# One encoder layer on one core: the mixer's output projection as seven half-size products in place of eight

## The chip, the cores and the metric

The kernel runs on one core of one Trainium2 chip. The metric is the device time of one execution in microseconds, given as the median of several runs. The profile is one more execution, recorded instruction by instruction. TensorE (PE) multiplies matrices, VectorE (DVE) and ScalarE (ACT) work element by element, GpSimd (POOL) does so as well and issues the DMAs that add one block in SBUF to another, and SyncE (SP) issues nearly all other DMAs.

## The reference

One layer over 512 rows of width 1024, in float32:

```python
u = rms_norm(h, g_mix[i])
z = u @ w_in[i]
...
gates = jax.nn.sigmoid(gate_logits).reshape(B, S, N_BRANCH, D_MODEL)
mixed = gates[:, :, 0] * y_a + gates[:, :, 1] * y_b
h = h + mixed @ w_mix_out[i]
u = rms_norm(h, g_mlp[i])
h = h + jnp.square(jax.nn.relu(u @ w_ff1[i])) @ w_ff2[i]
ple_gate = jax.nn.sigmoid(rms_norm(h, g_ple[i]) @ w_ple_gate[i])
h = h + ple_gate * (p[i] @ w_ple_proj[i])
```

`y_a` and `y_b` are two attention branches, each 512x512, projected to 1024 columns. The line that changes is `mixed @ w_mix_out[i]`, a product of 512x1024 with 1024x1024. A last RMS norm ends the layer.

## The kernel before

Every matrix product is done in three matmuls: each operand is split into a high part, rounded by ACT to TensorE's fast float32 format, and a low part, which DVE finds by subtracting (`hi_lo`, L68). `mm3` (L73) multiplies high by high, high by low and low by high. Weights are split in the same way, one "unit" of 128x1024 at a time (`emit_split`, L301). A list `order` holds all units in the order in which TensorE uses them; `advance` (L328) splits units up to a number, and `look["n"]` is the next one. Each unit's weights come from a "raw" block that SP loads into one of a few places. A planner (L189 to L226) gives each raw block the place that comes free first, and `emit_dma` (L246) issues a load only when the split of the last unit that used the place before has been issued. PE and POOL run in the order in which the program is written; ACT and DVE do so only inside `manual_schedule` blocks, and elsewhere the tile framework orders them.

Two parts of the layer already use Strassen's scheme in Winograd's form: the right half of each of the two gates and the MLP. There a product of 2x2 blocks takes seven block products in place of eight, numbered 1, 2, 5, 6, 7, 3 and 4. Their operands are sums of blocks. The sums of weights are made in place by `sum_source` (L276): POOL issues a DMA that adds one raw block to another (L298), or DVE adds them (L296). Product 5's weights are block 00 plus block 01; product 6's are those plus block 11; 7's are block 01 plus block 11, in place of block 01; 4's are those of 6 plus block 10. So each sum waits until the split of the unit before it has read the block. The results are gathered in three PSUM banks x, y and z: 6, 7 and 4 are added into the bank of 1, and 3 into that of 5, so the outputs are taken from the banks as they stand at that moment.

The stages around the change, in TensorE's order, are:

- branches 0 to 3 (`branches`, L1003): 24 matmuls for each block of 128 columns; DVE multiplies the PSUM results by the gates (L1016), adds the two (L1017) and splits the sum into an operand of the output projection (`mix_t`, L895);
- 14 gate products (`win_mm`, L906), then branches 4 to 7;
- the output projection, 8 output tiles of 128x512. For each, `row_group` (L1059) runs over 8 row blocks of `w_mix_out`, 3 matmuls each. `h2` (L1190) adds the tile to h (`h_add`, L1070) and lets ACT square it (`part_ssq`, L1081). When both halves of a 128-row block are done, `scale2` (L1194) finds 1/rms on POOL and scales the block on DVE, `t2_pe` (L1133) transposes it on PE, and `t2_top` (L1158, blocks 0 and 1) or `t2_sums` and its successors (L1166 to L1188, blocks 2 and 3) make the MLP's operands out of it;
- `pp_half` (L1210): the PLE projection `p @ w_ple_proj`, 8 tiles of 6 matmuls. It lies between the last tile of the output projection and the MLP, with the transposes of blocks 2 and 3 among it;
- the MLP: `steps` (L112) is a list of products in the order of `STEPS` (L46), where a and b are the first and second of a pair of 512 hidden columns in the first matrix (24 matmuls of 128x256 a product), A and B the same in the second (12 of 128x512).

The raw blocks of the output projection were 4 of 1 MB. The first MLP block had a place of its own ("t2"), free from the start of the projection.

Of the kernel before, what the change touches and what calls it, by code (L numbers as in the profile page):

```python
# [45 lines left out]
STEPS = "a1 b1 a2 a5 b5 b2 a6 b6 a7 a3 b7 b3 A1 a4 b4 B1 A2 A5 B5 B2 A6 B6 A3 A7 B7 B3 A4 B4"  # L46
ET = mybir.EngineType
# [3 lines left out]
def layer_kernel(ctx: ExitStack, tc: tile.TileContext, x, p, g_mix, w_in, b_forget, swa_sinks,  # L51
# [52 lines left out]
    def block(w, r0, c0, nk, nc_, name):  # L104
# [8 lines left out]
             for fq in range(4) for c, pn in STEPS.split()]  # L113
# [44 lines left out]
    for half in range(2):  # L158
        for r4 in range(2):
            for j, u in enumerate(rows(w_mix_out, r4 * 512, half * 512, f"wmix{half}{r4}")):  # L160
                add(("mix", half, 2 * r4 + j), u)
    for half in range(2):
        add(("pp", half), rows(w_ple_proj, 0, half * 512, f"wpp{half}", 2)[0])
    first_ff = len(raws)
    ff_blocks = {}
    for g in range(8):
        ff_blocks["f1", g] = block(w_ff1, 0, g * 512, 4, 256, f"wf1_{g}")
        ff_blocks["s2", g] = block(w_ff2, g * 512, 0, 2, 512, f"wf2_{g}")
# [61 lines left out]
    def ff_place(pl, shape):  # L230

        key = pl[:2] if isinstance(pl, tuple) else pl
        if key not in ff_tiles:
            if isinstance(pl, tuple):

                for z in range(2):
                    ff_tiles[pl[0], z] = (look["wp2"] if pl[0] else wp).tile(
                        [P, 2, 1024], F32, tag="w2_raw" if pl[0] else "w_raw", bufs=2,
                        name=f"wq{z}")
# [6 lines left out]
    def emit_dma(i):  # L246

        upto = max(first_raw[r] for r in raws_of(i))
        while look["d"] <= upto:
# [4 lines left out]
            if first_ff <= r_ < last_ff:  # L254
                if "place" not in look:
                    return
# [19 lines left out]
    def sum_source(i):  # L276
# [22 lines left out]
        sources[i] = q if key[0] == "s2" else q.rearrange("q k (j c) -> q k j c", c=P)  # L299

    def emit_split(i):  # L301
# [19 lines left out]
        for a in range(np_):  # L321
# [3 lines left out]
            nc.vector.tensor_tensor(lo[:, z], src[:, z], hi[:, z].bitcast(F32), ALU.subtract)  # L325
# [567 lines left out]
    mix = [None] * 8  # L893

    def mix_t(m):  # L895

        for i in (m // 2, 4 + m // 2):
            if mix[i] is None:
                mix[i] = at2.tile([P, 2, S], F32R, tag=f"d{i}", name=f"mix_{i}")
        return mix[m // 2][:, m % 2], mix[4 + m // 2][:, m % 2]  # L900

# [101 lines left out]
    def branches(m):  # L1003
# [8 lines left out]
        for i in range(2):  # L1012
            ps = mm_tile(f"psy{i}_{m}")
# [3 lines left out]
        nc.vector.tensor_tensor(sig[0], sig[0], sig[1], ALU.add)  # L1017
        hi_lo(*mix_t(m), sig[0])
# [3 lines left out]
    for t in P2_STEPS:  # L1022
# [12 lines left out]
        for n in range(look["n"], i + 9):  # L1035
            sum_source(n)
# [481 lines left out]
```

## Time and profile before

| | |
|---|---|
| median of 3 runs | 716.11 us (715.39 to 716.51) |
| span of the profiled execution | 715.3 us, granted clock 0.997 |
| PE busy | 704.4 us, 98% |
| DVE, ACT, POOL busy | 532.7, 450.2 and 84.8 us |
| DMA | 115.67 MB, 162 GB/s in the mean |

The profiled execution has no time of its own beside its span. The span runs from the first to the last instruction; the runs' median lies 0.8 us above it. Rows of the trace give the start, the duration, the engine, the line in the kernel and the operation as output<-inputs; `[... <-X]` is how long the engine stood idle before it and what ended that. A matmul's recorded duration overlaps the next one's, so its cost is the distance between starts. Weight units are named by number: u43 to u50 are those of the output projection before, with h for the high and l for the low part.

### The profile page before, as it was taken

The page shows a single profiled execution, that of the slowest core. Times are in us where ns is not written, and L with a number is a line of the kernel's source. Part 1 is how long each engine was busy: PE and PEld are TensorE (multiplying, and loading weights), DVE is VectorE, ACT ScalarE, POOL GpSimd, SP SyncE. Part 2 cuts the span into 40 slices and gives each one's busy share as a digit, 9 for nine tenths or more (in the row PEclk, how much of TensorE's full clock was granted, in tenths as well). Part 3 has the DMA queues.
Part 4 walks back from the last instruction along what each step waited for, and adds up shares of the span by engine and source line. Part 5 has one row for each costly group of instructions (what it writes and reads, how often), then busy time and mean ns, then how long its engine had stood idle before and what let it go on. Part 6 is the DMA issues. An engine that isn't in the chain of part 4 may idle for free.

```text
span 715.3 us, 11466 instructions
## 1 busy us (share of the span) xinstructions
PE 704.4 (98%) x4229; PEld 626.4 (88%) x4229; DVE 532.7 (74%) x908; ACT 450.2 (63%) x839; POOL 84.8 (12%) x124
## 2 busy tenths in 40 slices
PE   8999999999999999999999999999999999999995
PEld 7988888888888998888899889988999789988885
DVE  6557888877696556545789985899579966997565
ACT  6547888779863554344788736874477546875452
POOL 1011211100001200001510102010300021010101
PEclk9999999999999999999999999999999999999998
DMA  9256456670364795450885598739894699079002
GB/s 288 70 164 159 115 125 158 151 196 1 119 206 118 147 320 181 152 172 31 238 188 193 111 288 160 239 86 256 185 253 119 152 243 233 34 148 351 3 22 96
DMA packets 74055, 115.67 MB, mean 162 GB/s; under 512 B 6664, under 2 KB 44560, under 8 KB 74000
## 3 DMA queue, kind: packets, MB, share of 16 engines
q1 hardware_dynamic: 65936, 86.24, 38.0%
q0 software_dynamic: 7776, 28.32, 21.5%
q8 instruction: 33, 0.54, 0.3%
q10 hardware_dynamic: 288, 0.39, 0.2%
q14 instruction: 22, 0.18, 0.1%
HBM read 72.93 MB, written 4.19 MB: 108 GB/s over the span
## 4 chain that ended last, share of the span: by engine, by line
PE 86%; DVE 6%; DMA 4%; issue 2%; ACT 1%; POOL 0%; SPq 0%; POOLq 0%; DVEq 0%; ACTq 0%
PE pf L74 5%; PE pf L76 5%; PE pf L75 5%; PE s_6x L1331 3%; PE s_0x L1331 3%; PE h_sc L760 3%; PE s_2x L1331 2%; PE h_pv L830 2%; PE h_tr L818 2%; PE psm L76 2%; PE psm L74 2%; PE psy L74 2%; PE psy L75 2%; PE psm L75 2%; PE psy L76 2%
## 5 line engine op out<-in xcount | busy, mean ns | idle before, releaser
L298 POOL DMA_DIRECT2D wq<-wq x24 | 21.8, 936 | 166.8 <-DVE u70l L325 25.9
L778 ACT ACTIVATE s<-s,h_nm 128x128 f32<-128x128 f32 (+1 forms) x64 | 32.6, 512 | 5.9 <-DVE h_nm L771 5.1
L71 DVE TENSOR_TENSOR h_ptl<-h_tr,h_pth 128x512 fp32r<-128x512 f32 (+2 forms) x40 | 22.9, 604 | 4.0 <-ACT h_pth L70 3.6
L359 POOL TENSOR_SCALAR n_ms<-acc 128x1 f32<-128x1 f32 x15 | 5.6, 373 | 163.8 <-ACT junk L1083 105.4
L70 ACT CAST h_pth<-h_tr 128x512 fp32r<-128x512 f32 (+2 forms) x40 | 19.4, 523 | 1.8 <-PE h_tr L818 1.4
L70 ACT CAST u<-n_tr 128x512 fp32r<-128x512 f32 (+2 forms) x26 | 12.6, 519 | 11.8 <-PE n_tr L1139 5.6
L474 PE MATMUL va<-wv_h,u 128*128 128x320 f32 x64 | 20.0, 317 | 0.0
L818 PE MATMUL h_tr<-ident,s 128*128 128x128 f32 x136 | 19.6, 277 | 0.2
L474 PE MATMUL vb<-wv_h,u 128*128 128x328 f32 x64 | 19.6, 313 | 0.0
L71 DVE TENSOR_TENSOR u<-n_tr,u 128x512 fp32r<-128x512 f32 (+2 forms) x26 | 15.0, 603 | 5.8 <-ACT u L70 5.7
L298 POOL DMA_DIRECT2D wgw<-wgw x8 | 7.1, 971 | 102.3 <-DVE u25l L325 77.7
L1083 ACT ACTIVATE junk<-h_sb 128x512 f32<-128x512 f32 x16 | 10.1, 630 | 12.6 <-DVE h_sb L1073 10.1
L830 PE MATMUL h_pv<-h_pth,v 128*128 128x256 f32 (+1 forms) x64 | 17.3, 291 | 0.0
L830 PE MATMUL h_pv<-h_ptl,v 128*128 128x256 f32 (+1 forms) x64 | 16.9, 305 | 0.3 <-DVE h_ptl L71 0.3
L818 PEld LDWEIGHTS h_tr<-ident,s 128*128 128x128 f32 x136 | 15.1, 141 | 2.0 <-ACT s L798 0.5
L1420 DVE TENSOR_TENSOR sgp<-sgp,pp 128x512 f32<-128x512 f32 (+1 forms) x9 | 5.7, 632 | 14.2 <-ACT sgp L1419 14.2
L1073 DVE TENSOR_TENSOR h_sb<-psm,h_sb 128x512 f32<-128x512 f32 x8 | 5.5, 689 | 13.8 <-PE psm L76 13.8
L798 ACT ACTIVATE s<-s,h_rec 128x128 f32<-128x128 f32 (+2 forms) x32 | 14.2, 483 | 2.4 <-DVE h_rec L792 2.4
L840 DVE TENSOR_TENSOR h_ao<-h_pv,h_ao 64x512 f32<-64x512 f32 x16 | 10.9, 681 | 6.0 <-ACT h_ao L839 5.8
L766 DVE CUSTOM_DVE_ANT_0 s<-h_sc,causal 128x128 f32<-128x128 f32 (+3 forms) x32 | 13.8, 483 | 0.3 <-PE h_sc L760 0.3
L792 DVE RECIPROCAL h_rec<-h_den 128x4 f32<-128x4 f32 x16 | 3.0, 185 | 14.5 <-ACT s L778 14.3
L830 PEld LDWEIGHTS h_pv<-h_ptl,v 128*128 128x128 f32 x64 | 12.1, 188 | 1.7 <-DVE h_ptl L71 0.8
(1609 smaller groups left out, 2774.9 us busy)
## 6 DMA issues: line engine op xcount, KB each, us to landing
wq<-in_w_ff_dram SPq DMA_DIRECT2D x45, 512.0 KB, 5.9
wq<-wq POOLq DMA_DIRECT2D x24, 512.0 KB, 5.9
wq_c<-in_w_ff_dram SPq DMA_DIRECT2D x9, 512.0 KB, 6.7
wg<-in_w_in_dram SPq DMA_DIRECT2D x4, 1024.0 KB, 5.3
wgw<-in_w_in_dram SPq DMA_DIRECT2D x8, 512.0 KB, 4.7
wgw<-wgw POOLq DMA_DIRECT2D x8, 512.0 KB, 5.8
wmix<-in_w_mix_out_dram SPq DMA_DIRECT2D x4, 1024.0 KB, 5.1
wpg<-in_w_ple_gate_dram SPq DMA_DIRECT2D x4, 1024.0 KB, 8.6
```

Source lines behind the costliest of these rows:

```text
L70: nc.scalar.copy(hi, src)
L71: nc.vector.tensor_tensor(lo, src, hi.bitcast(F32), ALU.subtract)
L74: nc.tensor.matmul(ps, lh, rh, start=start, stop=False)
L75: nc.tensor.matmul(ps, lh, rl, start=False, stop=False)
L76: nc.tensor.matmul(ps, ll, rh, start=False, stop=stop)
L298: nc.gpsimd.dma_start(q, other, accum_op=ALU.add)
L474: nc.tensor.matmul(ps, u[:, kk_, ts_], w[:, kk_, c0:c1], start=kk_ == 0 and n == 0, stop=kk_ == KT - 1 and n == 2)
L760: nc.tensor.matmul(ps[:, off:off + n], qs[i][z][:, qb * P:(qb + 1) * P], kk[i][z][:, k0:k0 + n], start=z == 0, stop=z == 1)
L778: nc.scalar.activation(sl, sl, AF.Exp, bias=nm[:, qb:qb + 1], accum_out=den[:, qb:qb + 1])
L818: nc.tensor.transpose(tr[:, n, :], c["s"][:, o, :], ident)
L830: nc.tensor.matmul(pv[:, q0:q0 + nq, :], V2[kb][:, c["v"], :], t[:, o:o + nq, :], start=n == 0, stop=n == 2 * NT - 1, skip_group_check=True)
L1331: nc.tensor.matmul(bank[g // 2, "2" + bk, i], o, w, start=tg != "" and n == 0, stop=n == 5, skip_group_check=True)
```

## The change

The output projection becomes two groups of seven products. Group A takes rows 0 to 511 of `w_mix_out`, B rows 512 to 1023; each is cut into 2x2 blocks of 256 rows by 512 columns, and the rows of `mixed` into two halves. A product is two 128-row blocks times two 128-row weight blocks in three matmuls: 12 matmuls of 128x512. B adds to the banks that A has begun, and after each product of B its output goes into h. In `MIX_STEPS`, p0 and p4 stand for the units of the PLE projection.

The operands: `branches` no longer splits. For the first four column blocks POOL adds the two gated halves; `mix_sum` makes the four sums of blocks on POOL, for A during the gate products and for B during A1 and A2; `mix_ops` splits. Of the 14 weight units and the two of PLE, six have their low part made by POOL (`POOL_LO`). Eight sums of weights (four for each group) become DMAs issued by POOL. A unit is split two products ahead of its use. The loads of the MLP's first blocks now wait for the places of the projection's blocks, as the place "t2" holds p first. ACT and DVE run in written order from the start of the projection. The PLE projection's first tile goes between B7 and A4, seven after B4; rows 0 and 1 of h are normalised during p0 and A4, rows 2 and 3 after B4. In the MLP's first quarter b2 comes ahead of a5, and two weight sums of its first part go from DVE to POOL. `put` (L1144) is rewritten so that all high parts come ahead of the low parts.

The diff, cut to its core:

```diff
+STEPS_0 = STEPS.replace("a2 a5 b5 b2", "a2 b2 a5 b5")
+MIX_STEPS = "A1 A2 B1 A5 B2 B5 A6 B6 A3 B3 A7 B7 p0 A4 B4 p4"
+POOL_LO = [("mx", g, pn) for g, pn in ((0, 2), (0, 3), (1, 3), (0, 7), (1, 7))] + [("pp", 1)]
...
+    for g in range(2):
+        ff_blocks["mx", g] = block(w_mix_out, g * 512, 0, 2, 512, f"wmx_{g}")
+    for t in MIX_STEPS.split():
+        if t[0] != "p":
+            key = ("mx", "AB".index(t[0]))
+            add(key + (int(t[1]),), (ff_blocks[key], int(t[1]), [P, 2, 512]))
...
-                free_at.update({"t2": 0, "c6": late_places, "c7": late_places,
-                                "gb": late_places})
+                free_at.update({"t2": late_places, "c6": late_places,
+                                "c7": late_places, "gb": late_places})
...
-            if key[0] == "s2" and pn in (5, 7) or key in (("f1", 1, 6), ("f1", 1, 7)):
+            if key in (("f1", 1, 6), ("f1", 1, 7)):
+                nc.gpsimd.tensor_tensor(q, q, other, ALU.add)
+            elif key[0] == "s2" and pn in (5, 7):
                 nc.vector.tensor_tensor(q, q, other, ALU.add)
             else:
                 nc.gpsimd.dma_start(q, other, accum_op=ALU.add)
...
-            nc.vector.tensor_tensor(lo[:, z], src[:, z], hi[:, z].bitcast(F32), ALU.subtract)
+            on_pool = order[i][0] in POOL_LO
+            (nc.gpsimd if on_pool else nc.vector).tensor_tensor(lo[:, z], src[:, z], hi[:, z].bitcast(F32), ALU.subtract)
...
-        nc.vector.tensor_tensor(sig[0], sig[0], sig[1], ALU.add)
-        hi_lo(*mix_t(m), sig[0])
+        e, j = m // 2 % 2, m % 2
+        if m < 4:
...
+            nc.gpsimd.tensor_tensor(r_whole[e][:, j], sig[0], sig[1], ALU.add)
+            return
+        for i in range(2):
...
+            nc.vector.tensor_tensor(r_[1, i, e][:, j], sig[0][:, sl], sig[1][:, sl], ALU.add)
...
+    def mix_sum(g, n):
+
+        r11, r12, r21, r22 = (r_[g, i, e] for i in range(2) for e in range(2))
+        o, a, b, op = ((r22, r22, r21, ALU.subtract), (r21, r11, r21, ALU.subtract),
+                       (r11, r22, r11, ALU.add), (r12, r11, r12, ALU.subtract))[n]
+        nc.gpsimd.tensor_tensor(o, a, b, op)
...
+        terms = [(n, i, o[:, j, i * P:i * P + P], w[:, j, :]) for i in range(2)
+                 for n, (o, j, w) in enumerate([(oh, j, w) for j in range(2) for w in (wh, wl)]
+                                               + [(ol, j, wh) for j in range(2)])]
+        if key[-1] == 5:
+            terms.sort(key=lambda t: t[0] > 3)
...
+    man.enter_context(tc.manual_schedule(engines={ET.Activation, ET.DVE}))
+    for t in MIX_STEPS.split():
+        if t == "B5":
+            mix_ops(1, (3,))
...
+        if done[:1] == "B":
+            mix_out(int(done[1]))
+        if t == "p4":
+            break
+        if t == "A5":
+            mix_ops(1, (5,))
+        if t == "B2":
+            mix_ops(1, (7, 6))
+        if t == "B3":
+            p_transposed()
+        if t == "p0":
+            scale2(0)
+        key = ("mx", "AB".index(t[0]), int(t[1])) if t != "p0" else ("pp", 0)
+        if t == "A4":
+            scale2(1)
+        if t == "B4":
+            t2_pe(0)
+            new_u2()
+            t2_top(0)
+        advance(min(unit_of[key] + 2, f1_0 - 1))
...
+        if t in ("A1", "A2"):
+            mix_sum(1, 0 if t == "A1" else 2)
+            mix_sum(1, 1 if t == "A1" else 3)
+        if t == "p0":
+            pp_put(0, pp_mm(0))
+        else:
+            rows_mm("mx", t[0] == "A", MIX_TAGS, key, mix_op[key[1:]])
+        done = t
...
+    t2_pe(1)
+    ps = pp_mm(1)
+    t2_top(1)
+    scale2(2)
+    scale2(3)
+    pp_put(1, ps)
+    pp_put(2, pp_mm(2))
+    pp_put(3, pp_mm(3))
+    advance(f1_0)
     t2_pe(2)
     t2_sums(2)
+    pp_put(4, pp_mm(4))
+    advance(f1_0 + 1)
+    t2_pe(3)
     t2_sums2(2)
```

More of the change, by code (lines that the diff above doesn't have):

```diff
@@ L112, in layer_kernel @@
     steps = [("f1" if c in "ab" else "s2", 2 * fq + (c in "bB"), int(pn))
-             for fq in range(4) for c, pn in STEPS.split()]
+             for fq in range(4) for c, pn in (STEPS if fq else STEPS_0).split()]
     def add(key, spec):
@@ L157, in layer_kernel @@
             add(t, (gw[t[1]], t[3], [P, 4, 2, P]))
[L158 to L163, printed above, removed]
     first_ff = len(raws)
     ff_blocks = {}
+    for g in range(2):
[4 more added lines that the diff above has]
+            add(key + (int(t[1]),), (ff_blocks[key], int(t[1]), [P, 2, 512]))
+        elif t[1:] in "04":
+            half = int(t[1:]) // 4
+            add(("pp", half), rows(w_ple_proj, 0, half * 512, f"wpp{half}", 2)[0])
     for g in range(8):
@@ L1228, in layer_kernel @@
[L1228 to L1245 removed]
+        if half == 0:
+            pp_out.append(at2.tile([P, D], F32, tag=f"d{tb}", name=f"ppo_{tb}"))
@@ L1401, in layer_kernel @@
         done = st_
-        if n == 2:
+        if n == 3:
             man.close()
```

245 lines of the change are left out of this document (138 added, 107 removed).

## The prediction

> **What bounds the kernel now.** I read the cores first (one core, clock 0.997), then the page's busy shares, the windows cut at the borders of the stages, the chain that ended last, the waits of TensorE, and the timelines of the other engines around the output projection.
>
> ```profile
> span 715.3 us, 11466 instructions
> PE 704.4 (98%) x4229; PEld 626.4 (88%) x4229; DVE 532.7 (74%) x908; ACT 450.2 (63%) x839; POOL 84.8 (12%) x124
> PE 86%; DVE 6%; DMA 4%; issue 2%; ACT 1%; POOL 0%; SPq 0%; POOLq 0%; DVEq 0%; ACTq 0%
> ```
> ```profile
> 231.80:271.50 39.70, 39.70 (x338) 39.70 (x337) 22.18 (x23) 22.17 (x35) 5.19 (x6) 1.00 0.87 238
> 271.50:293.20 21.70, 21.70 (x97) 17.97 (x97) 13.83 (x18) 6.63 (x9) 0.00 (x0) 1.00 0.37 122
> 293.20:339.60 46.40, 46.40 (x222) 38.77 (x222) 24.64 (x33) 19.84 (x36) 2.62 (x6) 1.00 0.39 125
> 339.60:352.30 12.70, 12.70 (x63) 10.59 (x62) 9.83 (x16) 8.95 (x18) 6.67 (x7) 1.00 0.73 192
> 352.30:393.10 40.80, 40.80 (x349) 40.32 (x348) 36.43 (x39) 33.72 (x49) 4.82 (x5) 1.00 0.77 212
> ```
>
> The windows give length, then busy time of PE, weight loads, DVE, ACT and POOL, then granted clock, DMA share and GB/s. They are: the 14 gate products, the last four branch groups, the output projection with the transposes among it, the rest up to the MLP, and the MLP's first products. In all five PE is busy to the end and the clock is 1.00. So each matmul that goes is time gained, and each wait that comes is time lost; the other engines have room (DVE 24.64 of 46.40 us, POOL 2.62). The question is only whether the new feeding keeps up.
>
> **What is removed.** Before, each of 8 output tiles takes 8 row blocks of 3 matmuls: 192 of 128x512. After, 14 products take 12 each: 168. The MLP's second half holds products of the very same form:
>
> ```profile
> 396.03 2.72 PE s_0y L1331 x12
> 338.27 0.87 PE n_tr L1139 x8
> ```
>
> Twelve take 2.72 us, 0.227 us each. 24 fewer are worth 24 x 0.227 = **5.4 us**, on the path in full. The transposes (8 take 0.87 us) and the 48 matmuls of the PLE projection stay. Nothing makes more than 5.4 us likely, as PE has no idle time here that could be won.
>
> **What is added, where it is hidden.** Prices:
>
> ```profile
> 314.74 1.06 ACT L324 CAST u49h<-wmix 128x1024 fp32r<-128x1024 f32 x1 [0.30 <-PE psm L76]
> 359.44 1.23 DVE L325 TENSOR_TENSOR u57l<-wq,u57h 128x1024 fp32r<-128x1024 f32 x1
> 360.58 1.22 DVE L325 TENSOR_TENSOR u58l<-wq,u58h 128x1024 fp32r<-128x1024 f32 x1
> 298.88 0.69 DVE L1073 TENSOR_TENSOR h_sb<-psm,h_sb 128x512 f32<-128x512 f32 x1 [1.15 <-PE psm L76]
> 343.22 0.60 ACT L70 CAST u<-u_s 128x512 fp32r<-128x512 f32 x1
> 343.86 0.69 DVE L71 TENSOR_TENSOR u<-u_s,u 128x512 fp32r<-128x512 f32 x1 [0.76 <-ACT u L70]
> 348.25 1.35 POOL L1173 TENSOR_TENSOR u_s<-u_a,u_a 128x512 f32<-128x512 f32 x1
> 349.56 1.31 POOL L1183 TENSOR_TENSOR u_s<-u_a,u_s 128x512 f32<-128x512 f32 x1
> ```
>
> In a queue that is full these follow one another 1.1 us (1024 wide, DVE, 359.44 to 360.58) and some 0.6 us (512 wide) apart. Six more weight units cost ACT 6 x 1.06 = 6.4 us; their low parts cost DVE nothing, since six low parts go to POOL. Six more activation operands cost ACT 6 x 0.60 and DVE 6 x 0.69 us, six more additions into h another 6 x 0.69 = 4.1 us of DVE. ACT goes to some 30, DVE to some 33 of 41 us: hidden by PE as totals. The 4 + 4 activation sums on POOL (1.3 us each) fall in the gates, where POOL is busy 5.19 of 39.70 us, or ahead of products five steps later; uncovered, each would cost its 1.3 us. The MLP's first weights lose their early place and load when A7 and B7 have been split, about 325 us, some 15 us ahead of their use. Two MLP weight sums go from DVE to POOL, and b2 comes ahead of a5; with DVE at 36.43 of 40.80 us this can only ease DVE. I cost both at nothing; if either were late, its lateness would be the price.
>
> **Where the queues get tight.** I write the products as the change does and start them at 293.2, 2.72 us apart, so B6 would start at 312.2 and A3 at 315.0. A product needs the low part of its weights at its second matmul, 0.23 us in.
>
> First, B6, the product with the shortest notice. B5 is only two steps ahead of it. DVE must first add B1 into h (PE done at 301.4, two of 0.69 from 0.25 us later, as 298.88 follows the tile done at 298.64: 302.9), then make an operand's low part (0.6, and 0.7 allowed for POOL's sums beside it: 304.2), then the low part of B5's weights: 305.4. Only then may POOL issue B6's sum, a DMA that adds one block to another in place. Its price:
>
> ```profile
> wgw<-wgw POOLq DMA_DIRECT2D x8, 512.0 KB, 5.8
> 432.52 1.75 POOL L298 DMA_DIRECT2D wq<-wq  x2 [5.76 <-DVE u84l L325]
> 437.21 1.06 ACT L324 CAST u87h<-wq 128x1024 fp32r<-128x1024 f32 x1 [1.53 <-DMA wq<-wq]
> 435.00 0.86 POOL L298 DMA_DIRECT2D wq_t<-wq  x1 [0.72 <-DVE u85l L325]
> 442.52 1.05 ACT L324 CAST u88h<-wq_t 128x1024 fp32r<-128x1024 f32 x1 [2.40 <-DMA wq_t<-wq]
> ```
>
> From POOL's issue to ACT's reading it took 4.7 us (432.52 to 437.21) with little queued, 7.5 us (435.00 to 442.52) behind others, 5.8 in the median. The projection's DMA share was 0.39, and by the new places no weights are due to load between some 290 and 320 us, so I take 4.7: issued at 305.7, landed 310.4, high part 311.4, low part 312.6, against 312.5: **0.2 us** of wait; 1.3 with 5.8, 3.0 with 7.5.
>
> Second, A3, the first of four products in a row (A3, B3, A7, B7) whose low part is POOL's. Ahead of it in POOL's queue stands the DMA for B4's sum, which waits for B6's low part (312.6) and takes 0.9 us to issue with 0.3 ahead of it: 313.8. The trace has no POOL operation of 128x1024. Twice the shortest 128x512 is 2.6 us, twice the mean of the first sum's row is 3.0, and twice the longest, below, 3.9; below 2.6 I see no reason. I take 2.8, near the undisturbed rows: 316.6, against 315.4 for A3's second matmul: **1.3 us** (1.1 to 2.4). The next three, at 2.8 against steps of 2.72 with p's transposes (0.87) between, add 0.1.
>
> Third, behind B4. Row blocks 2 and 3 of h now both end with the last product. PE has one block's transposes and three PLE groups (0.87 + 3 x 1.36 = 5.0 us) before it needs the third block normalised. DVE and ACT need: 0.25, two additions (0.69 each, second done at 1.5), two squares on ACT behind them (0.63 + 0.19), done at 2.3, then the copies of the second block out of PSUM, the fourth of which ends at 2.3 + 0.27 + 0.95 + 0.6 = 4.1, its low part (0.6), 4.7, and then the scaling of the third block (1.4):
>
> ```profile
> 327.43 0.27 ACT L70 CAST u<-n_tr 128x128 fp32r<-128x128 f32 x1 [4.44 <-PE n_tr L1139]
> 328.35 0.95 ACT L70 CAST u<-n_tr 128x384 fp32r<-128x384 f32 x2
> 329.53 1.42 DVE L369 SCALAR_TENSOR_TENSOR n_xn<-h_sb,n_rs,g_mlp_bc 128x512 f32<-128x512 f32 x2 [1.51 <-POOL n_rs L362]
> 322.26 0.63 ACT L1083 ACTIVATE junk<-h_sb 128x512 f32<-128x512 f32 x1 [3.85 <-DVE h_sb L1073]
> 322.80 0.19 ACT L1083 ACTIVATION_READ_ACCUMULATOR junk<-h_sb 128x1 f32 x1
> ```
>
> That is 4.7 + 1.4 = 6.1 against 5.0: **1.1 us**. If ACT finds the copies sooner it falls to 0; if the squares of the fourth block come late as well, some 2.
>
> PLE's first group reads weights that load into a place freed by A7's low part (322.2). That load took 3.4 us before (5.9 for an MLP block): landed 325.8, split by 328.0, needed at 328.2. Nothing, or 1.6 us with 5.9.
>
> ```profile
> wpp<-in_w_ple_proj_dram SPq DMA_DIRECT2D x2, 512.0 KB, 3.4
> wq<-in_w_ff_dram SPq DMA_DIRECT2D x45, 512.0 KB, 5.9
> ```
>
> **The sum.** -5.4 + 0.2 + 1.3 + 0.1 + 1.1 = -2.7 us, on a span of 715.3, so 712.6. The median of the runs, 716.1, lies 0.8 above that span; the forecast as a median is **713.4 us**.
>
> **A row that speaks against it, and a rule.** POOL and DVE got in each other's way once:
>
> ```profile
> 355.65 1.19 POOL L298 DMA_DIRECT2D wq<-wq  x1
> 356.22 1.94 POOL L1183 TENSOR_TENSOR u_s<-u_a,u_s 128x512 f32<-128x512 f32 x1
> L71 DVE TENSOR_TENSOR at_ff<-u_s,at_ff x4: 679/686/2167, 354.7 to 358.6; 128x512 fp32r<-128x512 f32 x4
> ```
>
> While POOL ran its sum from 356.22 to 358.16, a DVE low part that reads two SBUF tiles took 2.17 us instead of 0.69. The Trainium skill, "SBUF — State Buffer", section "Who interferes with whom", says that a VectorE instruction with two SBUF inputs and a GpSimd instruction that reads SBUF exclude each other: whichever comes second waits for the whole of the first. By that rule, the trace agrees: the 1.48 us more are about one POOL sum. In the forecast the rule costs little, because beside the four low parts DVE has mostly additions out of PSUM, which read one SBUF tile. It is the third rival below. As to the size, the Trainium skill, "GPSIMD Engine Reference", section "3.1 Elementwise — side-by-side cycle accounting", has 4497 ns for 2048 elements, so an estimate of 2.25 us for 1024: by it the sum would be 0.6 us better; no row here shows that width.
>
> **The rivals.** *All waits hidden*: PE stays full as it was, 715.3 - 5.4 + 0.8 = **710.7 us**. For it: PE hardly waited in the same products of the MLP, which are fed in the same way. Against: there the second product of a pair has three steps for its sum, here two. Chance 0.15.
>
> *Sums land late*: if the DMA adds take 7.5 us, as the row at 435.00 did, B6 waits 3.0 us and the sum is -5.4 + 3.0 + 1.4 + 1.1 = +0.1: **716.2 us**, no change. Against: in that row MLP weights were loading beside it. Chance 0.19.
>
> *POOL becomes the bound, slower than before*: if DVE's low parts of A4 and PLE's weights and POOL's low parts exclude each other in turn, POOL's takes 2.8 plus 1.1 to 1.2 of waiting, or 3.9 plus 1.2: 3.9 to 5.1 us. At 4.5 A3 waits 3.0, B3 1.8 less the 0.9 of the transposes, A7 and B7 1.8 each: 7.5, with the 1.3 of the other two places 8.8: +3.4, **719.5 us**. It decides from about 3.7 us for a low part, where the loss reaches 5.4. For it: the 2.17 us row; against: from A6 to B7 DVE's own order holds no low part from SBUF but those of PLE's first group and of A4. Chance 0.16.
>
> **How the numbers follow.** Forecast 0.50 (its own range 711.6 to 714.6). 0.2% is 1.4 us, about what a measurement of this kernel can tell. Faster: the forecast, the first rival and a little of the second, 0.66; same: most of the second, 0.19; slower: most of the third, 0.15. The range from 710.6 to 717.5 leaves out the third rival and a little below.
>
> **What would show it.** In the profile of after: 168 projection matmuls, 0.227 us apart where nothing waits; idle time of PE at B6 (released by ACT or DVE behind a POOL DMA), at A3 (by POOL's low part) and at the third block's transposes (by DVE's scaling), 2.7 us together; POOL's 128x1024 low parts at 2.6 to 3.0 us; MLP from about 349.6 us on (352.3 before) and the same length from there. Wrong: any wait of PE outside these places, low parts over 3.2 us, B6's sum landing over 6 us after its issue, or a clock below 1.00 in the projection.

## The result and the profile after

The changed kernel takes 722.89 us (722.45 to 725.0, median of 4), the kernel before 716.08 beside it: a ratio of 1.0102 (95% interval 1.0087 to 1.0117). It is slower by 6.8 us, where 2.7 less were forecast. These are the head of the page of after, and the windows cut at the start of A1, at 340, at the MLP's first and eighth product, and at 409 us (columns as in the prediction):

```profile
span 721.1 us, 11513 instructions
PE 702.6 (97%) x4205; PEld 623.7 (86%) x4205; DVE 552.3 (77%) x918; ACT 457.0 (63%) x851; POOL 130.4 (18%) x152
```
```profile
292.98:340.00 47.02, 43.80 (x198) 34.68 (x197) 32.23 (x38) 23.95 (x39) 25.73 (x19) 1.00 0.79 204
340.00:353.12 13.12, 11.89 (x61) 9.59 (x60) 10.75 (x16) 8.62 (x19) 4.55 (x7) 1.00 0.62 189
353.12:378.66 25.54, 21.18 (x169) 20.57 (x168) 23.13 (x24) 19.59 (x32) 13.57 (x10) 0.95 0.66 156
378.66:409.00 30.34, 30.34 (x214) 28.54 (x214) 26.34 (x32) 23.14 (x32) 1.72 (x2) 0.98 0.72 194
```

The 24 matmuls are gone (4229 to 4205), but TensorE is no longer full: it idles 4.45 us before the MLP and 4.36 us in the MLP's first seven products, which take 25.54 us; before, they took 19.13 (352.14 to 371.27) and TensorE idled in neither stretch. The last two windows show a clock below 1.00. TensorE's waits, the longest first:

```profile
PE ('f1', 0)x L918 <- DVE u65l L334: 3.1, 1, 3.1
...
PE n_tr L1194 <- DVE n_xn L378: 1.2, 1, 1.2
PE mxx L1302 <- DVE u50l L334: 0.8, 1, 0.8
PE ('f1', 1)y L918 <- DVE u62l L334: 0.8, 1, 0.8
PE n_tr L1194 <- DVE u L1218: 0.7, 1, 0.7
...
PE mxz L1302 <- POOL u51l L334: 0.5, 1, 0.5
PE mxx L1302 <- ACT u50h L332: 0.5, 1, 0.5
PE ('f1', 1)y L918 <- ACT u62h L332: 0.5, 1, 0.5
PE mxx L1302 <- DVE h_sb L1126: 0.4, 1, 0.4
PE pspp L78 <- DVE at_ff L334: 0.3, 1, 0.3
```

`u50` is B6's weight, `u51` A3's, `at_ff` under `pspp` the PLE weight, `u62` the MLP's b2, `u65` its a6; `n_tr` are the transposes of h's blocks and `mxx` under `h_sb` is A4's bank. The longest wait is at a6, in the MLP, where the prediction had put nothing. What VectorE and GpSimd do ahead of it:

```profile
366.79 3.50 DVE L1218 TENSOR_TENSOR at_ff<-u_s,at_ff 128x512 fp32r<-128x512 f32 x2
370.21 0.68 DVE L933 TENSOR_TENSOR u_('f1', 1)_4070<-('f1', 1)y,u_('f1', 1)_4070 128x512 f32<-128x512 f32 x1
370.81 2.28 DVE L1430 TENSOR_TENSOR o<-u_('f1', 0)_4042,o 128x512 fp32r<-128x512 f32 x1
```
```profile
366.96 2.78 POOL L302 TENSOR_TENSOR wq<-wq 128x1024 f32<-128x1024 f32 x1
369.70 2.84 POOL L302 TENSOR_TENSOR wq<-wq,wq 128x1024 f32<-128x1024 f32 x1
```

The two sums that the change gave to GpSimd run from 366.96 to 372.54. Beside them VectorE's two low parts take 3.50 us together and the next 2.28; undisturbed they take 1.28 and 0.68 (below). The operation between them, at 370.21, reads PSUM and one SBUF tile, and takes its normal 0.68. After the wait the clock falls:

```profile
366.00:371.00 5.00, 5.00 (x47) 5.00 (x46) 5.00 (x5) 2.92 (x5) 5.00 (x4) 1.00 0.90 170
371.00:374.80 3.80, 0.76 (x7) 0.55 (x5) 3.80 (x4) 3.80 (x8) 1.54 (x1) 1.00 0.28 54
374.80:378.80 4.00, 3.92 (x23) 3.92 (x24) 4.00 (x5) 1.77 (x2) 1.72 (x2) 0.67 0.61 116
378.80:382.00 3.20, 3.20 (x26) 3.20 (x25) 1.26 (x2) 1.54 (x3) 0.00 (x0) 0.88 1.08 187
```

TensorE is busy for 0.76 of 3.80 us, and then the granted clock is 0.67 and 0.88 for some 7 us. The 22 matmuls of a6 left at 374.88 take 3.8 us instead of 22 x 0.1135 = 2.5, and b6 3.2 instead of 2.7: 1.8 us more, on top of the wait.

Where the time lies, from the starts of the products (A1, the MLP's first, its eighth) in the profiled executions:

| kernel | A1 starts | A1 to the MLP | its first seven products | rest | span |
|---|---|---|---|---|---|
| before | 293.24 | 58.90 | 19.13 | 344.0 | 715.3 |
| after | 292.98 | 60.14 | 25.54 | 342.4 | 721.1 |
| MLP sums back on VectorE | 293.25 | 59.74 | 22.22 | 342.3 | 717.5 |
| no GpSimd arithmetic but group A's sums | 293.35 | 58.43 | 22.20 | 342.4 | 716.4 |
| that, and the weight place given back | 293.43 | 54.73 | 22.24 | 342.4 | 712.8 |

The last three rows are experiments. The spans differ by 5.8 us, the medians by 6.8. Per stretch, the change cost 1.2 us up to the MLP (-2.7 forecast), 6.4 in the MLP's first seven products (0 forecast), and the rest is 1.6 us shorter.

### The profile page after: what moved, and what is told of

It reads as the page before. It is cut to its first block, busy times and chain, and to the rows that moved or that the text cites. A ratio compares the mean times of both kernels' runs of the same rounds, so it can differ in the third digit from the quotient of the medians.

```text
span 721.1 us, 11513 instructions
## 1 busy us (share of the span) xinstructions
PE 702.6 (97%) x4205; PEld 623.7 (86%) x4205; DVE 552.3 (77%) x918; ACT 457.0 (63%) x851; POOL 130.4 (18%) x152
## 4 chain that ended last, share of the span: by engine, by line
PE 86%; DVE 5%; issue 3%; ACT 3%; DMA 1%; POOL 1%; POOLq 0%; DVEq 0%; ACTq 0%
PE pf L77 5%; PE pf L79 5%; PE pf L78 5%; PE (3, 's2')x L1302 3%; PE (0, 's2')x L1302 3%; PE (2, 's2')x L1302 3%; PE (1, 's2')x L1302 3%; PE h_sc L769 2%; PE h_pv L839 2%; PE h_tr L827 2%; PE psy L77 2%; PE psy L78 2%; PE psy L79 2%; PE vb L483 2%; PE va L483 2%
## 5 line engine op out<-in xcount | busy, mean ns | idle before, releaser
L306 POOL DMA_DIRECT2D wq<-wq x35 | 30.5, 933 | 160.8 <-DVE u43l L334 26.0
L1024 POOL TENSOR_TENSOR r_a<-gl,gl 128x512 f32<-128x512 f32 x4 | 6.1, 1526 | 83.8 <-ACT u25h L332 75.8
L306 POOL DMA_DIRECT2D wq_t<-wq x5 | 4.3, 862 | 62.1 <-DVE u104l L334 25.6
L1528 ACT ACTIVATE sgp<-psgt,rs 128x512 f32<-128x512 f32 x7 | 4.8, 686 | 14.6 <-PE psgt L79 14.6
L741 POOL TENSOR_SCALAR bswa<-dist 128x256 f32<-128x256 f32 x8 | 7.0, 881 | 37.6 <-DVE h_mx L775 36.5
L74 DVE TENSOR_TENSOR u<-n_tr,u 128x512 fp32r<-128x512 f32 x16 | 10.4, 683 | 4.1 <-ACT u L73 4.1
```

Source lines behind the costliest of these rows:

```text
L74: nc.vector.tensor_tensor(lo, src, hi.bitcast(F32), ALU.subtract)
L306: nc.gpsimd.dma_start(q, other, accum_op=ALU.add)
```

## The experiments

Theory L: a GpSimd operation that reads SBUF and a VectorE operation with two SBUF inputs exclude each other, so the MLP's two sums, moved to a slower engine, also hold VectorE. Rival Q: VectorE is short of time there anyhow, and giving it the sums back makes it later. A third idea, late weights, came up on the way. Each run is compared with runs of the kernel before beside it, 715.6 to 716.0 in the median.

**The MLP's two sums back on VectorE** (the change otherwise whole):

```diff
             if key in (("f1", 1, 6), ("f1", 1, 7)):
-                nc.gpsimd.tensor_tensor(q, q, other, ALU.add)
+                nc.vector.tensor_tensor(q, q, other, ALU.add)
```


> The change with the two MLP weight sums (products b6 and b7 of the first quarter) back on DVE. Theory L (POOL's additions of two SBUF tiles lock out DVE's): after the change DVE's operand low parts from 366.79 us took 3.50 instead of 1.29 and the next one 2.28 instead of 0.69, 3.8 us lost against 2.3 us of own work saved, so a6's weights come about 1.5 us sooner, PE's wait of 3.1 us there shrinks to about half and the slow clock behind it with it: 1.5 to 3 us less than after, 720 to 721.4. Theory Q (DVE's and ACT's written queues are simply late because two blocks of h are normalised last; POOL is incidental): DVE has 2.3 us more to do ahead of a6's weights, so 1 to 2.5 us more, 724 to 725.4.

719.18 us (718.93 to 719.34), ratio 1.0052 (1.0037 to 1.0067): 3.7 less than after. VectorE's rows at that place, the sums included:

```profile
367.25 1.21 DVE L302 TENSOR_TENSOR wq<-wq 128x1024 f32<-128x1024 f32 x1
368.38 1.22 DVE L302 TENSOR_TENSOR wq<-wq,wq 128x1024 f32<-128x1024 f32 x1
369.51 1.28 DVE L1218 TENSOR_TENSOR at_ff<-u_s,at_ff 128x512 fp32r<-128x512 f32 x2
370.72 0.68 DVE L1430 TENSOR_TENSOR o<-u_('f1', 0)_4042,o 128x512 fp32r<-128x512 f32 x1
371.32 1.22 DVE L334 TENSOR_TENSOR u65l<-wq,u65h 128x1024 fp32r<-128x1024 f32 x1
```

VectorE does 2.4 us more work and reaches a6's low part at 371.32 instead of 373.62. The wait at a6 is 1.0 us instead of 3.1, the clock stays full. For these two sums Q is out.

**GpSimd busy in two ways.** Two runs on top of that one: two needless 128x1024 operations on GpSimd that read two SBUF tiles, and 50 memsets of 128x16 that read none. Both stand behind the second sum, and the two operations of the first cancel:

```diff
+                if pn == 7:
+                    for o_ in (ALU.add, ALU.subtract):
+                        nc.gpsimd.tensor_tensor(other, other, q, o_)
...
+                if pn == 7:
+                    for _ in range(50):
+                        nc.gpsimd.memset(scr[0], 0.0)
```


> e1 (the MLP sums on DVE) with two more POOL operations of 128x1024 behind them that nothing needs: block 11 of those weights plus, and then minus, the summed block, so its value stays but for rounding. L: POOL reads two SBUF tiles for 5.6 us while DVE makes operand and weight low parts from SBUF; some of these grow to 2 us and more, a6's weights come 2 to 4 us later, and the time goes back toward that of the change: +2 to +4.5 us on e1 (721.2 to 723.7). Q: nothing waits for them but product b3's weights, four steps later: within 0.2% of e1 (719.2).

> e1 with 50 POOL memsets of 128x16 in the same place: POOL is busy for about 5 us there too, but reads nothing. If what holds DVE is POOL's reading of SBUF: no DVE operation grows and the time is that of e1 (719.2 within 0.2%). If any POOL activity on SBUF holds DVE, or if POOL's own lateness is what counts (its next weight sum, wanted by a4, is behind the memsets): +1 to +4 us.

Reading: 725.54 us (723.99 to 726.61), 6.4 more than without, and more than L expected; the low parts take 3.49 and 2.84 us, the wait at a6 is 5.1 and the clock falls to 0.50. Writing alone:

```profile
366.72 9.03 POOL L305 MEMSET scr<- 128x16 f32 x50
```
```profile
369.82 1.28 DVE L1221 TENSOR_TENSOR at_ff<-u_s,at_ff 128x512 fp32r<-128x512 f32 x2
371.02 0.68 DVE L1434 TENSOR_TENSOR o<-u_('f1', 0)_4043,o 128x512 fp32r<-128x512 f32 x1
```

GpSimd is busy 9.03 us and no VectorE operation grows. The time is 720.37 (719.86 to 720.92), 1.2 more, which both expectations would take, so the rows decide: the wait at a6 is 1.0 as without the memsets, and 0.5 us shows as a new wait further on. The next accumulating DMA is issued behind the memsets, at 376.22 instead of 372.83; that it makes this wait is not shown. So what holds VectorE is GpSimd's reading, not the occupation of GpSimd or of its queue. L is shown.

**The same move in the kernel before**:

```diff
-            if key[0] == "s2" and pn in (5, 7) or key in (("f1", 1, 6), ("f1", 1, 7)):
+            if key in (("f1", 1, 6), ("f1", 1, 7)):
+                nc.gpsimd.tensor_tensor(q, q, other, ALU.add)
+            elif key[0] == "s2" and pn in (5, 7):
```


> The kernel before with one part of the change alone: its two MLP weight sums (b6 and b7 of the first quarter) on POOL in place of DVE. There DVE did them at 361.72 us, two of 1.17. L: POOL's two of 2.8 us hold DVE's operations on two SBUF tiles for some 4 us in a stretch where DVE is full (36.4 of 40.8 us), so that one or two of the low parts between 362 and 372 us take 2 us or more; PE had those weights 2 to 4 us ahead, so it waits 0 to 2 us: 0 to +2 us on before, and more if a slow clock follows. Without a lock: DVE is eased, no operation grows, no change (within 0.2%).

716.81 us (716.16 to 719.13, 10 runs), ratio 1.0019 (1.0009 to 1.0029):

```profile
360.67 6.66 POOL L296 TENSOR_TENSOR wq<-wq,wq 128x1024 f32<-128x1024 f32 x2 [2.57 <-DVE u57l L327]
```
```profile
362.33 2.74 DVE L327 TENSOR_TENSOR u59l<-wq_t,u59h 128x1024 fp32r<-128x1024 f32 x1
365.00 2.89 DVE L1157 SCALAR_TENSOR_TENSOR at_ff<-u_s,at_ff 128x512 fp32r<-128x512 f32 x1
```

The same grip: VectorE loses 1.5 and 2.2 us on these two (1.22 and 0.69 undisturbed), while it is spared the sums' 2.4. Here 0.7 us of it reaches TensorE as a wait (for a bank that ACT copies, behind VectorE's late work), and 1.0 the time.

**The order of b2 and a5**:

```diff
-STEPS_0 = STEPS.replace("a2 a5 b5 b2", "a2 b2 a5 b5")
+STEPS_0 = STEPS
```


> The change with the MLP's first quarter in its old order (a5 and b5 ahead of b2). If the order makes b2's wait (1.3 us with what follows), it goes: 721.5 or less. L and Q alike: a5's operand is done at 362.0 us where it would be wanted at 361.4, so that it waits 0.7 to 1.5 us itself and nothing is won: 722 to 724.5.

722.55 us (721.28 to 724.31), as after; the waits at b2 (0.8 + 0.5 us) stand at a5 instead, now the fourth product, and the 3.1 us wait stands at b2's weight (3.2), now the sixth. The order is neutral.

**The clock**: 28 transposes of the identity on TensorE ahead of a6, their results unused:

```diff
+        if n == 6:
+            idle = psA.tile([P, 4, P], F32, tag="tr", bufs=3, name="idle")
+            for j in range(28):
+                nc.tensor.transpose(idle[:, j % 4, :], ident, ident)
```


> The change with 28 transposes of the identity on PE ahead of product a6 of the first quarter, 28 x 0.11 = 3.1 us of work whose result nobody reads, in the place of PE's wait of 3.1 us. After that wait the granted clock was 0.67 for 4 us and 0.88 for 3.2, worth 1.9 us. If the idle time brings the slow clock: the fill takes the wait's place, the clock stays at 1.00 and the time falls by 1 to 2 us (721 to 722). If the clock falls for another reason (load, the stage): same or up to 1 us more.

The clock stayed at 1.00 from 360 to 406 us, and the MLP's fourteenth product (`u72`) started at 394.60 instead of 395.98: 1.4 us of the 1.8 came back. But the run took 726.22 us (724.67 to 727.74), 3.3 more than after and outside both expectations. VectorE, done with `u72`'s low part 1.3 us sooner than in after, met a weight still under way, and TensorE waited 1.9 us at 409, with the clock down once more (0.77 and 0.74 to 416):

```profile
392.34 1.23 DVE L304 TENSOR_TENSOR wq_gb<-wq_gb,wq 128x1024 f32<-128x1024 f32 x1 [2.96 <-DMA wq<-in_w_ff_dram]
```

So the slow clock is a real part of the loss at a6, but taking it away alone gains nothing, since the weights come at their own pace (DMA share 0.94 to 1.14 from 378 to 390). Why this load came later than in after (where the sum ran at 390.64 unhindered) isn't settled.

**Low parts back on VectorE**, then **all GpSimd arithmetic but group A's sums** (low parts, the MLP's sums and group B's sums on VectorE):

```diff
-POOL_LO = [("mx", g, pn) for g, pn in ((0, 2), (0, 3), (1, 3), (0, 7), (1, 7))] + [("pp", 1)]
+POOL_LO = []
...
-                nc.gpsimd.tensor_tensor(q, q, other, ALU.add)
+                nc.vector.tensor_tensor(q, q, other, ALU.add)
...
-        nc.gpsimd.tensor_tensor(o, a, b, op)
+        (nc.vector if g else nc.gpsimd).tensor_tensor(o, a, b, op)
```


> The change with the low parts of all weight units back on DVE. L: the normalisation of the second block of h (3.58 us instead of 1.4 beside POOL's low part of PLE's second unit) is no longer held, nor do A3 to B7 hang on POOL's 2.4 to 2.7 us a unit; 1 to 3 us less than after, 720 to 722. Q: six more operations of 1.1 us in DVE's queue, 0 to 3 us more, 723 to 726.

> Both of the above, and group B's four operand sums on DVE: POOL keeps only DMAs and small sums in the projection. L: the gains of both together, 3 to 6 us less than after, 717 to 720. Q: 12 more operations on DVE, some 11 us of work in about 60 us, 2 to 6 us more, 725 to 729.

The first (only its first line) takes 723.39 us (722.6 to 724.59), no gain, and in Q's range rather than L's. The rows show no overfull VectorE, though: A3's wait is gone and the third block's is 0.3, but the PLE weight's load is late instead (1.4 and 0.8 us), with the clock at 0.62 behind it. The second takes 717.91 (717.17 to 718.31, 7 runs), ratio 1.0030 (1.0019 to 1.0042): the products follow one another without a wait up to B7, 2.3 us sooner than in after, and then TensorE waits again:

```profile
PE pspp L77 <- ACT at_ff L332: 1.3, 1, 1.3
...
PE n_tr L1194 <- DVE n_xn L378: 1.0, 1, 1.0
PE pspp L78 <- DVE at_ff L334: 0.8, 1, 0.8
```

ACT had stood ready for the PLE weight 3.62 us before it landed. Feeding the products faster had brought the next late thing forward: a load. So the seven-product form without GpSimd's help was still some 2 us slower than eight products, and the question was where its 5.4 us went.

**Four runs on that**: the PLE tile moved behind A4 (and the two normalisations one step along); b2's split ahead of a5's operand; both; and both with the low parts and group B's sums on GpSimd.

```diff
-MIX_STEPS = "... A7 B7 p0 A4 B4 p4"
+MIX_STEPS = "... A7 B7 A4 p0 B4 p4"
...
-    t2_rest(5)
     advance(f1_0 + 3)
+    t2_rest(5)
```


> The third experiment's kernel (no TENSOR_TENSOR of the change on GpSimd but group A's sums) with the PLE projection's first tile moved behind A4 (steps 'A7 B7 A4 p0 B4 p4', both normalizations one step along). It removes one wait alone: TensorE's 1.3 + 0.8 us for the PLE weights' high and low part, whose load lands late; A4's 12 matmuls (2.7 us) now lie ahead of it. Theory G (what is left of the loss is late weights, and each wait gives its time back): 715.4 to 716.6, pspp's waits under 0.4. Rival N (whatever is gained ahead of the MLP is held back again in the MLP's first quarter by weights that come at their own pace): 717.4 to 718.4, the waits gone but the MLP's a6, b6 or the first s2 later by as much.

> The third experiment's kernel with one line moved: the split of the MLP's fourth weight (b2's, which the change has put one place ahead) is issued before the left operand of a5 instead of behind it. It removes one wait alone: TensorE's 0.8 + 0.5 us at b2. Theory G (each wait gives its time back): 716.5 to 717.1, the waits at b2 under 0.3, none above 0.5 at a5. Rival N (passed on): 717.5 to 718.3, with the same time lost at a5 or a6.

> The third experiment's kernel with both: the PLE tile behind A4, and b2's split ahead of a5's operand. Theory G (waits add up): 714.0 to 715.8, so at or below the kernel before. Rival N: 717.0 to 718.3.

> As the run with both edits, but with the change's low parts and group B's sums on GpSimd kept (the MLP's two weight sums stay on VectorE). Theory L (a 128x1024 TENSOR_TENSOR of GpSimd holds VectorE's two-input operations and is itself 2.4 to 2.8 us late): 715.2 to 717.2, so 1.0 to 1.7 above the run with both, its waits at A3 and B6. Rival S (with the stage's other waits gone the splitting of the low parts between the engines pays, as VectorE has more time): equal to or below the run with both.

The first takes 718.95 us (718.24 to 720.79), 1.0 more, against both expectations. The PLE weight's low part still stood ahead of the additions into h in VectorE's queue, so A4 waited 4.2 us for its bank:

```profile
329.57 1.23 DVE L334 TENSOR_TENSOR at_ff<-wq,at_ff 128x1024 fp32r<-128x1024 f32 x1 [3.43 <-ACT at_ff L332]
330.71 1.28 DVE L1126 SCALAR_TENSOR_TENSOR h_sb<-mxx,h_sb 128x512 f32<-128x512 f32 x2
```

The tile had been a cover for that bank, and the late load hit the queue all the same. TensorE's clock fell to 0.50 behind this wait. The second takes 717.61 (717.21 to 718.9, 9 runs): the wait at b2 falls from 1.3 to 0.5 us and comes back at a6 (0.7 to 1.4), the seven products take 22.2 us as before. Passed on, as rival N had it. Both together: 719.85 (718.85 to 720.13), above both expectations, with the wait at A4's bank at 3.9. With GpSimd's arithmetic kept: 718.08 (717.81 to 719.74), 1.8 less, where L expected 1.0 to 1.7 more. There A4's wait is only 0.9, as TensorE comes later to it, so here the slower feeding pays: what GpSimd's arithmetic costs depends on what it delays.

**The weight place given back.** The change keeps p's raw tile in the place (`t2`) that was free for a weight before. Here p lies where the normalized rows come later, and the PLE projection's first weight takes the place:

```diff
             pl = min(free_at, key=free_at.get)
+            if raws[r]["name"].startswith("wpp0"):
+                pl, free_at["t2"] = "t2", 0
...
-            p_sb = wk3.tile([P, NT, 256], F32, tag="t2", bufs=1, name="p_sb")
+            p_sb = wk3.tile([P, NT, 256], F32, tag="xn", bufs=2, name="p_sb")
```


> The third experiment's kernel (no TENSOR_TENSOR of the change on GpSimd but group A's sums) with one buffer moved: p's raw tile lies where the normalized rows come later, instead of in the place for a weight that the change took from the loads, and the PLE projection's first weight is loaded into that place, so its load needn't wait until a block of the mixer's weight is split. The order on every engine stays. Theory W (the seven-product form loses most of its gain to late weights, because it holds one weight place less): TensorE's waits at pspp (1.3 + 0.8 us) go, the load is issued at least 3 us before 322.3, the MLP's first product starts 1.2 to 2.3 us earlier and the time is 715.4 to 717.0. Rival N (passed on to the MLP's a6, b6 and first s2): 717.4 to 718.4 with the MLP's start earlier all the same.

> The same buffer's move in the first experiment's kernel (low parts and group B's sums on GpSimd as in the change, the MLP's two weight sums on VectorE), where TensorE did not wait for the PLE weights, as it came to them 2.4 us later. Theory W as it stands says little: 718.4 to 719.4, no wait there to remove. If the place also lets the MLP's weights come sooner, 717.3 to 718.3 with the waits at b2 (1.3) and a6 (1.0) smaller. The p4 to MLP stretch shows which.

> The run before this, and b2's split ahead of a5's operand. With the split alone in its place in the kernel without GpSimd's arithmetic the time went from 717.9 to 717.6, so theory N expects 0 to -0.4 on the run before this. Theory S (GpSimd's low parts relieve VectorE in the third block, so that here the split finds room): -0.6 to -1.3.

With no GpSimd arithmetic but group A's sums: **714.57 us** (713.89 to 715.25, 11 runs), ratio 0.9981 (0.9972 to 0.9990), 3.3 less, and below the kernel before. SP's queue and TensorE's waits:

```profile
308.13 1.49 SPq L273 DMA_DIRECT2D wq_t<-in_w_ple_proj_dram  x1
```
```profile
PE ('f1', 1)y L920 <- DVE u62l L336: 0.8, 1, 0.8
PE ('f1', 0)x L920 <- DVE u65l L336: 0.7, 1, 0.7
...
PE n_tr L1196 <- DVE n_xn L380: 0.6, 1, 0.6
PE ('f1', 1)y L920 <- ACT u62h L334: 0.5, 1, 0.5
```

The load is issued 9.4 us sooner than the first PLE load of the run without it (317.54), and 12.1 sooner than the one that ACT stood waiting for there (issued at 320.20, landed 7.2 us later). No wait is left before the third block. A1 to the MLP takes 54.73 us, 4.2 less than before and 3.7 less than without the place. That is more than the 2.3 expected at most: the 2.1 us at `pspp` are gone, and of the waits behind it 0.4 at A4's bank and 0.4 at the third block as well. The waits at b2 and a6 are what they were, so nothing was passed on. Theory W is shown for this kernel. With GpSimd's low parts and group B's sums kept: 718.16 (717.52 to 719.84); b2's split first on top: 718.26 (717.42 to 719.76). There the place is worth 1.0 us, and the split nothing.

**What is left**: the MLP's sums by the accumulating DMA (no engine adds them), the same with b2's split first, and the low parts alone back on GpSimd.

```diff
-            if key in (("f1", 1, 6), ("f1", 1, 7)):
-                nc.vector.tensor_tensor(q, q, other, ALU.add)
-            elif key[0] == "s2" and pn in (5, 7):
+            if key[0] == "s2" and pn in (5, 7):
...
-POOL_LO = []
+POOL_LO = [("mx", g, pn) for g, pn in ((0, 2), (0, 3), (1, 3), (0, 7), (1, 7))] + [("pp", 1)]
```


> The run that gave the place back (714.57) with the MLP's two weight sums done by the accumulating DMA, as the other f1 sums are: neither VectorE's 1.21 + 1.22 us nor GpSimd arithmetic. In every run of this study with those sums on VectorE the MLP's first seven products take 22.2 us, and 19.1 in the kernel before; VectorE is busy for 0.93 of 352 to 375 us there. Theory D (VectorE's queue paces that stretch): its 2.4 us less bring the seven products to 20.0 to 21.5 and the time to 712.4 to 714.0. Rival T (the transfer is itself late: a sum landed 4.7 us after issue in the mixer): b6's or a6's wait grows, 714.5 to 717.

> The first of these runs with b2's split ahead of a5's operand. Where VectorE is relieved by 2.4 us the split finds room: theory D expects 0.3 to 1.0 below the first run (712.0 to 713.5); if b2's wait is only passed on to a6, as with VectorE's sums, within 0.4 of it.

> The run that gave the place back (714.57) with the change's six low parts on GpSimd again, group B's sums on VectorE. With low parts and group B's sums both on GpSimd the time was 718.16, so 3.6 more. Theory P (the low parts themselves are late, 2.4 to 2.8 us each where VectorE takes 1.2, and hold VectorE): 716.3 to 717.8, TensorE waiting at A3 and A4 but not at B6. Rival M (it is group B's sums, which stand in GpSimd's queue ahead of the issue of B6's accumulating DMA): 714.6 to 715.6.

By DMA: 719.74 us (718.87 to 720.46), with the split first 719.12 (718.47 to 720.61). The first is above both expectations; the two do not differ beyond their spread. Four such DMAs stand in one row at GpSimd, and VectorE, with less to do, waits for what they add:

```profile
359.95 3.52 POOL L306 DMA_DIRECT2D wq<-wq  x4 [5.09 <-DVE u63l L334]
```
```profile
370.97 1.22 DVE L334 TENSOR_TENSOR u66l<-wq,u66h 128x1024 fp32r<-128x1024 f32 x1 [2.30 <-ACT u66h L332]
```

The wait at b6 is 1.1 + 0.8 us, and the clock falls to 0.61. The seven products take 23.3 us, as rival T had it. Theory D gets no support, but it is not tested cleanly either: what VectorE is spared it spends waiting for what these DMAs add, and a6 still waits 0.8: its own sum, a DMA in every run, is read by ACT 4.8 us after its issue.

Low parts alone on GpSimd: 716.93 (715.88 to 718.79, 11 runs), 2.4 more than with them on VectorE. The time is theory P's; group B's sums are the other 1.2 of the 3.6. The places are P's only in part: 0.4 us shows at A3, nothing at A4, and more at the third block's transposes (1.2 instead of 0.6) and at a6 (1.4 instead of 0.7).

## Why the prediction was wrong

**The matmuls (-5.4)** were right: 24 are gone, and A1 to the MLP is 4.2 us shorter than before in the best run, where some waits are left.

**B6 (+0.2) and A3 (+1.3, and 0.1 behind it)**: B6 waited 1.3 us and A3 0.5. From the start of A6 to that of B3 it is 11.66 us, and 8.99 without GpSimd's arithmetic: 2.7 lost where 1.6 were priced. B6's sum was issued 1.2 us later than worked out, at 306.90: group B's sums on GpSimd (3.65 us for two of 128x512 at 301.87, not 2.6) held VectorE's operand and B5's low part, ahead of that issue, as rows of after show. ACT read the sum 4.8 us after its issue, straight behind its squares of h, so when it landed is not seen. Low parts took 2.4 to 2.7 us, near the 2.8 taken.

```profile
301.87 3.65 POOL L1064 TENSOR_TENSOR r_b<-r_b,r_b 128x512 f32<-128x512 f32 x2
```
```profile
301.97 2.39 DVE L74 TENSOR_TENSOR u_mix<-r_b,u_mix 128x512 fp32r<-128x512 f32 x1
304.29 2.32 DVE L334 TENSOR_TENSOR u48l<-wq,u48h 128x1024 fp32r<-128x1024 f32 x1
```

**The third block (+1.1)**: 1.2, but the size is met partly by luck. Another 0.7 us stands earlier, at the second block's transposes, a place that the prediction did not have. That block's scaling on VectorE, with its next low parts behind it, took 3.58 us beside GpSimd's low part of the second PLE unit; the first block's took 1.40:

```profile
335.28 3.58 DVE L378 SCALAR_TENSOR_TENSOR n_xn<-h_sb,n_rs,g_mlp_bc 128x512 f32<-128x512 f32 x2
```
```profile
335.61 2.71 POOL L334 TENSOR_TENSOR at_ff<-wq,at_ff 128x1024 fp32r<-128x1024 f32 x1 [8.09 <-ACT at_ff L332]
```

Without GpSimd's arithmetic the third block waits 1.0, and 0.6 in the best run.

**The PLE weights (nothing, or 1.6)**: the wait was seen, its size was not. In after the load was issued at 322.28, as worked out, and landed 5.4 us later, not 3.4. From B7's start to A4's it is 5.32 us, and 4.12 with the place given back: 1.2 us, of which 0.3 shows at `pspp` and 0.4 at A4's bank behind it. Without GpSimd's arithmetic TensorE comes 2.3 us sooner, and it is 2.1 us at `pspp`. That the loads had lost a place was noted for the MLP's weights and given no price; it was the cover of the PLE's, and giving it back was worth 3.3 us.

**The step that failed** is "Two MLP weight sums go from DVE to POOL ... this can only ease DVE. I cost both at nothing". It cost 3.7 us, the largest part of the 9.5 between forecast and result: some 2.1 us more of wait at a6 (3.1 against 1.0) and 1.8 by the clock. The stage's totals misled (36.43 of 40.80 us busy on VectorE): the price of an operation moved to GpSimd was counted by its own length, not by what it holds on VectorE.

**The third rival** had the right mechanism, priced in the wrong place. It put the exclusion between A3 and B7, where little of VectorE's work reads two SBUF tiles; it cost most in the MLP's first products, where most of it does, and where the change had put two more GpSimd operations. The rule of the Trainium skill, "SBUF — State Buffer", section "Who interferes with whom", that a VectorE instruction with two SBUF inputs contends with a GpSimd instruction that reads SBUF, not with one that only writes it, agrees with both halves of the test: 3.49 and 2.84 us beside reads, 1.28 and 0.68 beside memsets. What it would have made of the forecast is two VectorE stalls of up to 2.8 us each at a6, an estimate from the 2.8 us that the prediction took for a GpSimd operation of that size.

**The MLP's length (the same)**: wrong by 3.1 us or more in every run of the seven-product form (22.2 at best instead of 19.1). It is not that TensorE comes sooner to work done at the old pace: with the MLP's sums back on VectorE the MLP starts at 352.99, later than in the kernel before (352.14), and its first seven products take 22.2 us, as they do from 348.16 in the best run. What VectorE has to do for it moves along with its start. The low parts of the weights of a1, b1 and a2 begin 5.7 and 3.2 us ahead of that start and 2.9 behind it, in after and in the best run alike; in the kernel before, 13.9, 6.3 and 4.9 us ahead. Between them stand the sums and operands of h's blocks 2 and 3, both normalised behind the last product now.

GpSimd makes four sums for these, in both kernels, and in the best run three low parts of VectorE beside them (at 344.93, 351.04 and 354.07) take 2.34, 1.74 and 1.85 us instead of 1.22, 1.22 and 0.69, just ahead of b2's at 357.04; in the kernel before only one grows, by 1.5. a6's weights wait for their accumulating DMA as well: issued at 360.47 behind a5's split, read by ACT at 365.19 after 0.85 us of standing idle. Which of these paces the stretch stays open: no run changes where these two blocks are normalised or takes these sums off GpSimd, moving one split only passed the wait on, and taking sums off VectorE by DMA brought waits of its own.

Some 1.6 us come back behind the seven products in after (342.4 instead of 344.0), of which 1.2 is idle time of TensorE: 7.1 us from 409 to the end, and 8.3 from 401.3 in the kernel before, nearly all of it in the last 21 us. Why it is shorter isn't settled.

Undone step by step, the way down from 722.89 is: the MLP's sums 3.7, low parts and group B's sums 1.3, the place 3.3: 714.57, still 1.2 above the forecast. In another order the parts differ (with the place given back, low parts and group B's sums are 3.6, and the place 1.0 with them on GpSimd), since each wait removed uncovers another.

## What to carry to other kernels

Before moving an elementwise operation to GpSimd, list what VectorE runs in the same microseconds: beside VectorE's low parts, which read two SBUF tiles, a GpSimd operation that reads SBUF as well cost up to 2.2 us (operations of 2.4 to 3.3 us here), and totals of busy time don't show it. When a TensorE-bound stage is shortened, its loads and operands lose time that the old length had covered: check every place and transfer, first of all where the change takes a buffer. Undo one part at a time, but expect the parts not to add up: here a run with one wait removed was slower twice, as another late item took the time.

## What the runs showed of the hardware

TensorE's granted clock fell behind waits of 2 to 3 us. As the mean of the windows that were cut, it fell to 0.67 behind 3.1 us of waiting (after), to 0.62 behind 1.4 + 0.8 us (low parts back on VectorE), to 0.61 behind 1.1 + 0.8 us (the sums by DMA) and to 0.77 behind 1.9 us (the run with transposes of the identity), but not behind 1.0 us, nor behind 1.3 + 0.8 us in another run:

```profile
328.00:331.00 3.00, 1.56 (x7) 0.95 (x6) 0.23 (x1) 1.30 (x2) 0.00 (x0) 1.00 1.06 377
331.00:334.00 3.00, 2.24 (x6) 1.58 (x6) 3.00 (x4) 0.92 (x2) 0.00 (x0) 0.62 0.42 114
```
```profile
328.00:331.50 3.50, 1.90 (x6) 1.05 (x6) 2.97 (x4) 1.45 (x2) 0.00 (x0) 1.00 0.53 160
331.50:335.00 3.50, 3.36 (x18) 2.86 (x19) 3.08 (x5) 3.48 (x7) 0.00 (x0) 1.00 0.84 273
```

The first pair is the run with the low parts back on VectorE, the second the run without GpSimd arithmetic, at the same place. In after the drop costs 1.4 to 1.8 us on top of the wait. The Trainium skill, "TensorE: Matmul & The Clock Gate", section "Part 1: The HAM clock gate (the "warmup" mystery)", has the clock go to half after an idle window of some 3.4 us. The half agrees with the lowest windows here (0.50 behind waits of 4.2 and 5.1 us); the length does not, as two waits of 2.2 and 1.9 us in all, with work between, were enough in two runs. What decides is not shown: ahead of a drop TensorE was busy 1.56 of 3.00 us, and 1.90 of 3.50 where none came.
